# Bounded gathers, a deferred combination and repacked operands in a hybrid retention, S5 and mixture-of-experts block

## The chip, the cores and the metric

The kernel runs on one core of a Trainium2 chip. The metric is the device time of one execution in microseconds (us). The engines are PE (matrix products), DVE (vector), ACT (scalar functions and scaled copies), POOL (GpSimd) and SP, which only issues transfers; 16 DMA engines move the data. Each engine and each queue works its own list of instructions in order and waits on the others through semaphores.

## The reference, cut to what matters

512 tokens of width 2048, float32 throughout. A mixer (retention beside an S5 state space model) adds to x; a mixture of 32 experts adds to x; a gated projection (PLE) adds to x; a norm ends it.

```python
# S5: states of 64 groups of 16 channels, 64 complex states each
y = real(einsum('gcp,bsgp->bsgc', c_mat, states))
# router: 4 groups and 32 experts, 36 logits per token
g_prob = softmax(ht @ w_rg + b_rg);  e_logits = ht @ w_re + b_re
...
top_logit, top_j = lax.top_k(e_sel, 2)          # two experts of the best group
e_w = softmax(top_logit) * g_w
# each of the 1024 assignments goes through its expert
a = silu(xb @ w_gate[e]) * (xb @ w_up[e])        # 2048 -> 512
y = a @ w_down[e]                                # 512 -> 2048
out = segment_sum(y * row_w, row_tok)
# PLE
x = x + sigmoid(h @ w_ple_gate) * (p @ w_ple)
```

## The kernel before

Up to about 1350 us the program runs the mixer: dense products in three passes of split operands (L103, L104, L105: high by high, high by low, low by high; L62 on ACT makes the high part, L63 on DVE the low one), with the small products of the S5 part between them. `add_cross` (L467) multiplies the states xst of eight blocks of groups with the weights wb; xst holds chunk, part and group in that order, so one product reads every 64th element of a row.

The output projection goes over four blocks cb of 512 columns. After each, x is transposed (pt, L744), copied to SBUF (xt, L746, by ACT and DVE in turn), and multiplied by the router's weights wr (pl, L748), in two halves of 64 columns by parity of the piece. Each product of two float32 operands is two records in the trace and one row in the order of instructions.

Then the routing: `dispatch_ids` (L855 to L862) multiplies one-hot matrices ohd by token numbers (pq), so that each of the 128 slots of a pair of experts (64 each) holds its token number plus one, or zero where the slot is empty. The gather (L862, POOL) brings one row of 2048 numbers of x from HBM to each partition of xo; an empty slot brings row 0. `dispatch_scales` (L871) gives the weights sw, `dispatch_part` (px, L885) transposes xo into xg. Between these, PE makes the 32 products pw of p with w_ple, which wait for evacuation by ACT and a store to pw_d (L993 to L997).

The experts run in 16 pairs. Per expert, `load_expert` loads eight tiles of 1 MB for gate and up (L703) and four for down (L712) through SP's queue into 13 buffers mw and mwx, which are used in turn. `expert` makes pg (L1010; 64 slots by 512 columns, eight records per tile, in two halves of the array), sg on ACT and DVE (L1013 to L1015), pt and aT (L1018, L1020), py (L1026) and from it ysh on ACT and ysl on DVE (L1033, L1034), in split form. `combine` multiplies both by one-hot matrices (pc, L1049; 32 products for a pair), and DVE adds each result to x (L1050). The 16 px for the next pair stand in the first expert of a pair. The order on PE follows from a scheduler that knows the written order and the readiness of operands.

At the end `gate_w` (L1060 to L1068) loads and splits the first weights of the PLE gate: wh on ACT (L1066), wl on DVE (L1067), twelve times 128x512 each for the three tiles that are made early. A loop for experts with more than 64 tokens (L1105) follows, which begins with a branch on every engine, and then the PLE products (L1167 on).

## Time and profile before

| | us |
|---|---|
| median of 3 runs | 2581.95 (2581.84 to 2582.83) |
| profiled execution | 2583.66 |
| its span | 2581.9 |
| PE busy in the span | 2454.1 (95%) |
| DVE busy | 1128.8 (44%) |
| ACT busy | 570.2 (22%) |
| POOL busy | 133.6 (5%) |
| data moved | 626.41 MB, mean 243 GB/s |

The page's shares are means over stretches of different kinds; the table of stages among the rows below separates them. Ends of products are modelled, so the pace of PE is best read from the starts of neighbouring records.

### The profile page before, as it was taken

The page shows a single profiled execution, that of the slowest core. Times are in us where ns is not written, and L with a number is a line of the kernel's source. Part 1 is how long each engine was busy: PE and PEld are TensorE (multiplying, and loading weights), DVE is VectorE, ACT ScalarE, POOL GpSimd, SP SyncE. Part 2 cuts the span into 40 slices and gives each one's busy share as a digit, 9 for nine tenths or more (in the row PEclk, how much of TensorE's full clock was granted, in tenths as well). Part 3 has the DMA queues.
Part 4 walks back from the last instruction along what each step waited for, and adds up shares of the span by engine and source line. Part 5 has one row for each costly group of instructions (what it writes and reads, how often), then busy time and mean ns, then how long its engine had stood idle before and what let it go on. Part 6 is the DMA issues. An engine that isn't in the chain of part 4 may idle for free. (4 is left out here: it accounts for less than half of the span.)

```text
span 2581.9 us, 27822 instructions
## 1 busy us (share of the span) xinstructions
PE 2454.1 (95%) x11178; PEld 1595.3 (62%) x11178; DVE 1128.8 (44%) x2204; ACT 570.2 (22%) x722; POOL 133.6 (5%) x166
## 2 busy tenths in 40 slices
PE   8999999999999999999998999999999999997998
PEld 7888788888888888887763333333333333333886
DVE  6647966333443343542223344343333333334435
ACT  4242222231221232222221110000000000012534
POOL 1010000001101100000001000000000000000101
PEclk9999999999999999999999999999999999998999
DMA  8332333443323334653348999999999999995334
GB/s 300 110 99 90 120 117 103 152 161 104 106 90 98 104 124 148 224 218 114 116 172 344 421 420 421 420 420 421 420 421 421 420 420 421 421 420 231 104 118 147
DMA packets 168228, 626.41 MB, mean 243 GB/s; under 512 B 16402, under 2 KB 25106, under 8 KB 115490
## 3 DMA queue, kind: packets, MB, share of 16 engines
q1 hardware_dynamic: 160112, 597.22, 60.4%
q0 software_dynamic: 3376, 19.01, 1.8%
q10 hardware_dynamic: 4610, 8.39, 0.9%
q8 instruction: 89, 1.46, 0.2%
q14 instruction: 41, 0.34, 0.0%
HBM read 595.21 MB, written 29.43 MB: 242 GB/s over the span
## 5 line engine op out<-in xcount | busy, mean ns | idle before, releaser
L63 DVE TENSOR_TENSOR wl<-wst,wh 128x2048 fp32r<-128x2048 f32 (+1 forms) x111 | 251.6, 2267 | 410.7 <-ACT wh L62 410.5
L62 ACT ACTIVATE wh<-wst 128x2048 fp32r<-128x2048 f32 (+1 forms) x111 | 207.4, 1869 | 603.8 <-PE acc L104 359.1
L103 PE MATMUL acc<-hTh,wh 128*128 128x512 f32 x832 | 327.9, 394 | 11.2 <-ACT wh L62 6.8
L104 PE MATMUL acc<-hTl,wh 128*128 128x512 f32 x832 | 328.5, 395 | 0.0
L105 PE MATMUL acc<-hTh,wl 128*128 128x512 f32 x832 | 326.0, 393 | 0.3 <-DVE wl L63 0.2
L1010 PE MATMUL pg<-mw,xg 128*64 128x512 f32 x1040 | 259.6, 596 | 0.0
L1010 PE MATMUL pg<-mwx,xg 128*64 128x512 f32 x1008 | 250.6, 597 | 0.2 <-issue 0.2
L103 PEld LDWEIGHTS acc<-hTh,wh 128*128 128x128 f32 x832 | 157.1, 189 | 46.1 <-ACT wh L62 7.8
L1050 DVE TENSOR_TENSOR x<-pc,x 128x512 f32<-128x512 f32 x256 | 162.0, 685 | 41.0 <-PE pc L1049 40.7
L105 PEld LDWEIGHTS acc<-hTh,wl 128*128 128x128 f32 x832 | 157.3, 189 | 33.7 <-DVE wl L63 1.8
L104 PEld LDWEIGHTS acc<-hTl,wh 128*128 128x128 f32 x832 | 157.2, 189 | 32.9 <-issue 0.8
L1034 DVE SCALAR_TENSOR_TENSOR ysl<-py,sw,ysh 64x512 fp32r<-64x512 f32 x128 | 94.7, 749 | 175.5 <-ACT ysh L1033 170.8
L1010 PEld LDWEIGHTS pg<-mw,xg 128*64 128x64 f32 x1040 | 76.9, 137 | 139.9 <-issue 139.6
L1014 DVE SCALAR_TENSOR_TENSOR sg<-pg,sw,sg 128x256 f32<-128x256 f32 x32 | 15.5, 483 | 324.7 <-ACT sg L1013 324.7
L1010 PEld LDWEIGHTS pg<-mwx,xg 128*64 128x64 f32 x1008 | 73.7, 137 | 135.3 <-issue 135.1
L1033 ACT ACTIVATE ysh<-py,sw 64x512 fp32r<-64x512 f32 x128 | 87.3, 682 | 312.9 <-PE py L1026 298.4
L1026 PE MATMUL py<-mw,aT 128*64 128x512 f32 x616 | 147.3, 622 | 5.7 <-DVE aT L1020 5.7
L1013 ACT ACTIVATE sg<-pg,sw 128x256 f32<-128x256 f32 x32 | 15.1, 473 | 570.0 <-PE pg L1010 570.0
L1049 PE MATMUL pc<-ysh,oht 128*128 128x512 f32 x256 | 108.4, 433 | 29.1 <-ACT ysh L1033 22.3
L1049 PEld LDWEIGHTS pc<-ysh,oht 128*128 128x128 f32 x256 | 49.0, 192 | 100.6 <-DVE x L1050 54.5
L1049 PE MATMUL pc<-ysl,oht 128*128 128x512 f32 x256 | 101.7, 407 | 0.4 <-DVE ysl L1034 0.4
L103 PE MATMUL accp<-wh,h3h 128*128 128x512 f32 x256 | 101.6, 397 | 0.0
(354 smaller groups left out, 3618.9 us busy)
## 6 DMA issues: line engine op xcount, KB each, us to landing
mw<-in_w_exp_gu_dram SPq DMA_DIRECT2D x130, 1024.0 KB, 19.8
mwx<-in_w_exp_gu_dram SPq DMA_DIRECT2D x126, 1024.0 KB, 19.7
mw<-in_w_exp_down_dram SPq DMA_DIRECT2D x77, 1024.0 KB, 19.8
mwx<-in_w_exp_down_dram SPq DMA_DIRECT2D x51, 1024.0 KB, 19.8
wst<-in_w_in_dram SPq DMA_DIRECT2D x39, 1024.0 KB, 5.1
wst<-in_w_merge_dram SPq DMA_DIRECT2D x32, 1024.0 KB, 5.7
wst<-in_w_out_dram SPq DMA_DIRECT2D x16, 1024.0 KB, 5.3
wst<-in_w_ple_gate_dram SPq DMA_DIRECT2D x16, 1024.0 KB, 5.2
```

What stands on the lines that cost most here:

```text
L62: S.activation(hi, src, AF.Copy)
L63: V.tensor_sub(lo, src, hi.bitcast(FT))
L103: PE.matmul(acc, s0, m0, start=first, stop=False)
L104: PE.matmul(acc, s0, m1, start=False, stop=False)
L105: PE.matmul(acc, s1, m0, start=False, stop=last)
L1010: PE.matmul(pg[hf * 64:(hf + 1) * 64, :], xk, gu[kt // 2][:, kt % 2, :, hf * 256:(hf + 1) * 256], start=kt == 0, stop=kt == 15)
L1014: V.scalar_tensor_tensor(sg, pg[:, 0:256], rcol, sg, op0=OP.mult, op1=OP.mult)
L1026: PE.matmul(pys[c2][ch * 64:(ch + 1) * 64, :], aT[:, kc % 2, (kc // 2) * 64:(kc // 2 + 1) * 64], dn[kc][:, c0:c0 + 512], start=kc == 0, st ...
L1033: S.activation(yh[q, c0:c0 + 512], pys[c2][q], AF.Copy, scale=wcol[q])
L1034: V.scalar_tensor_tensor(yl[q, c0:c0 + 512], pys[c2][q], wcol[q], yh[q, c0:c0 + 512].bitcast(FT), op0=OP.mult, op1=OP.subtract)
L1049: PE.matmul(pc, oh[cb // 2][:, i * 128:(i + 1) * 128], ys[n][:, sl], start=n == 0, stop=n == 1)
L1050: V.tensor_tensor(x2[i][:, sl], pc, x2[i][:, sl], op=OP.add)
```

## The change

- `add_cross`: ACT copies the states of a block into contiguous xc, which the products then read.
- Router: wr is split into a high and a low part, side by side in 72 columns; x transposed is split too (ACT and DVE); eight products per block of 512 columns take the place of four of float32. The square for the norm is written over its input in PSUM.
- Gather: xo is one buffer, cleared once on POOL; an empty slot's index lies beyond a bound given to the gather, which is to leave out such rows.
- Experts: the combination of a pair is called in the middle of the next pair's first expert, the transposes of the next pair's rows in the middle of the second expert, and the scheduler places both among the other products.
- PLE: for the three early tiles ACT also scales the weights in place and POOL makes the difference; the last combination is written after them.
- The clearing of the routing table moves from the start to a later place on POOL.

```diff
+        xc = [t2k([128, BP, NCH], f"xc{i}") for i in range(2)]
+        for i in range(2):
+            S.activation(xc[i].rearrange("p j n -> p n j"), xst[:, 0:NCH, i, js], AF.Copy)
         py = ps("py")
         pyv = py.rearrange("p (j x) -> p j x", x=128)
         for jj in range(BP):
             for i in range(2):
-                PE.matmul(pyv[:, jj, :], wf[i][:, jj, :], xst[:, 0:NCH, i, j0 + jj], start=i == 0, stop=i == 1)
+                PE.matmul(pyv[:, jj, :], wf[i][:, jj, :], xc[i][:, jj, :], start=i == 0, stop=i == 1)
...
+    tini = glu.tile([128, (E * CAP + 2 * T) // 128, 4], FT, name="tini", bufs=1)
+    GP.memset(tini, 0.0)
+    GP.memset(tini[:, :, 0], -1.0)
+    GP.dma_start(tbl_d.rearrange("(p n) f -> p n f", p=128), tini)
...
-    wr = x1pool.tile([128, 16, 64], FT, name="wr", bufs=1)
-    GP.memset(wr[:, :, 36:], 0.0)
-    nc.sync.dma_start(wr[:, :, :36], A["w_router"])
-    GP.tensor_tensor(wr[:, :, :36], wr[:, :, :36], nffn[:, :, None].to_broadcast([128, 16, 36]), op=OP.mult)
+
+    wr = x1pool.tile([128, 16, 72], FR, name="wr", bufs=1)
+    wrf = wpool.tile([128, 4, 512], FT, name="wrf", tag="wst").rearrange("p k c -> p (k c)")[:, :576] \
+        .rearrange("p (d e) -> p d e", e=36)
+    nc.sync.dma_start(wrf, A["w_router"])
+    GP.tensor_tensor(wrf, wrf, nffn[:, :, None].to_broadcast([128, 16, 36]), op=OP.mult)
+    S.activation(wr[:, :, 0:36], wrf, AF.Copy)
+    V.tensor_tensor(wr[:, :, 36:72], wrf, wr[:, :, 0:36].bitcast(FT), op=OP.subtract)
...
-            jk = opool.tile([128, 512], FT, name="jk", tag="xt")
-            S.activation(jk, xn, AF.Square, accum_out=ss2[:, i, cb:cb + 1])
+            S.activation(p, xn, AF.Square, accum_out=ss2[:, i, cb:cb + 1])
...
-            xt = opool.tile([128, 512], FT, name="xt", tag="xt")
-            (S.activation(xt, pt, AF.Copy) if d % 2 else V.tensor_copy(xt, pt))
-            o = (d % 2) * 64
-            PE.matmul(pl[o:o + 64, :], wr[:, cb * 4 + d, :], xt, start=d < 2, stop=d >= 2)
+            xt = [opool.tile([128, 512], FR, name="x" + n, tag="x" + n) for n in "hl"]
+            split(pt, *xt)
+            for n in range(2):
+                PE.matmul(pl[:72], wr[:, cb * 4 + d, :], xt[n], start=d == n == 0, stop=d == 3 and n == 1)
...
+    xo = xtile([128, D], "xo", "xo")
+    GP.memset(xo, 0.0)
...
-        tk1 = mo.tile([128, 2], FT, name="tk1")
+        tk1 = mo.tile([128, 2], FT, name="tk1", bufs=3)
         V.tensor_reduce(tk1, pq[:, 0:4].rearrange("p (v n) -> p v n", v=2), axis=mybir.AxisListType.X, op=OP.add)
         oi = mo.tile([128, 1], I32, name="oi")
-        V.tensor_scalar(oi, tk1[:, 0:1], -1.0, 0.0, op0=OP.add, op1=OP.max)
-        xo = xtile([128, D], "xo", "xo")
+        none = mo.tile([128, 1], FT, name="none")
+        V.tensor_scalar(none, tk1[:, 0:1], 0.0, 2.0 * T, op0=OP.is_equal, op1=OP.mult)
+        V.scalar_tensor_tensor(oi, tk1[:, 0:1], -1.0, none, op0=OP.add, op1=OP.add)
         GP.indirect_dma_start(out=xo, out_offset=None, in_=x1_d,
-                              in_offset=bass.IndirectOffsetOnAxis(ap=oi[:, 0:1], axis=0))
+                              in_offset=bass.IndirectOffsetOnAxis(ap=oi[:, 0:1], axis=0),
+                              bounds_check=T - 1, oob_is_err=False)
...
+        if mid:
+            mid()
...
-        yh, yl = ys
+        yh, yl = ys()
...
+                if early:
+                    S.activation(st[:, k, :], st[:, k, :], AF.Copy, scale=sc)
+                    GP.tensor_tensor(wl[:, k, :], st[:, k, :], wh[:, k, :].bitcast(FT), op=OP.subtract)
+                    continue
...
     sw = sw0
+    last = None
     for pr in range(E // 2):
         _, xo, xg, tk1, _ = disp
         nxt, sw_n = disp, sw
-        ys = ytiles()
+        ys = []
+
+        def get_ys():
+            if not ys:
+                ys.extend(ytiles())
+            return ys
         for e in range(2):
             ee = pr * 2 + e
             wts = load_expert(wgu_a[ee], wd_a[ee]) if ee else first
+            for d4 in range(0 if ee else 4):
+                dispatch_part(xo, xg, d4)
             if e == 0 and pr + 1 < E // 2:
                 nxt = dispatch_ids(pr + 1)
                 sw_n = dispatch_scales(nxt[0], pr + 1)
 
             def xcol(kt):
-                if ee == 0 and kt % 4 == 0:
-                    dispatch_part(xo, xg, kt // 4)
                 return xg[:, kt, e * CAP:(e + 1) * CAP]
-            expert(wts, xcol, sw[:, e, 1:2], sw[:, e, 0:1], ys, e)
-            if e == 0 and pr + 1 < E // 2:
-                for d4 in range(4):
-                    dispatch_part(nxt[1], nxt[2], d4)
+
+            def mid():
+                if e == 0 and last:
+                    combine(*last)
+                if e == 1 and pr + 1 < E // 2:
+                    for d4 in range(4):
+                        dispatch_part(nxt[1], nxt[2], d4)
+            expert(wts, xcol, sw[:, e, 1:2], sw[:, e, 0:1], get_ys, e, mid)
         disp = nxt
         sw = sw_n
-        if pr == E // 2 - 1:
-            right = False
-            mwx.release()
-            x1pool.release()
-            ple = tc.alloc_tile_pool(name="ple", bufs=1, side="right", reuse_waits="tile")
-            pre = [gate_w(q, 0, q, mtile().rearrange("p (k c) -> p k c", k=4)) for q in range(3)]
-        combine(ys, [tk1[:, v:v + 1] for v in range(2)])
-
+        last = ys, [tk1[:, v:v + 1] for v in range(2)]
+    right = False
+    mwx.release()
+    x1pool.release()
+    ple = tc.alloc_tile_pool(name="ple", bufs=1, side="right", reuse_waits="tile")
+    pre = [gate_w(q, 0, q, mtile().rearrange("p (k c) -> p k c", k=4)) for q in range(3)]
+    combine(*last)
```

Line numbers move by the change: L1010 becomes L1022, L1018 L1032, L1026 L1040, L1034 L1048, L1049 L1063, L1050 L1064, L855 L864, L862 L872, L871 L882, L1066 L1081, L1067 L1084 (POOL).

On PE, in the experts, from the end of a pair's py, the order before was this (pc: combination of the pair that ends, pg: first expert of the next):

```order
L1049 MATMUL pc<-ysh,oht 128x512
L1010 MATMUL pg<-mwx,xg 64x512
L1049 MATMUL pc<-ysl,oht 128x512
L1049 MATMUL pc<-ysh,oht 128x512 x2
L1049 MATMUL pc<-ysl,oht 128x512 x2
L1049 MATMUL pc<-ysh,oht 128x512
L1049 MATMUL pc<-ysl,oht 128x512
L1049 MATMUL pc<-ysh,oht 128x512
L1049 MATMUL pc<-ysl,oht 128x512
L1049 MATMUL pc<-ysh,oht 128x512
L1049 MATMUL pc<-ysl,oht 128x512
L1010 MATMUL pg<-mwx,xg 64x512 x2
```

It is now this, with pq for the next gather ahead of py instead of among pg:

```order
L1040 MATMUL py<-mw,aT 64x512 x16
L1063 MATMUL pc<-ysh,oht 128x512
L1022 MATMUL pg<-mw,xg 64x512 x4
L1063 MATMUL pc<-ysl,oht 128x512
L1063 MATMUL pc<-ysh,oht 128x512
L1063 MATMUL pc<-ysl,oht 128x512
L1063 MATMUL pc<-ysh,oht 128x512
L1063 MATMUL pc<-ysl,oht 128x512
L1063 MATMUL pc<-ysh,oht 128x512
L1022 MATMUL pg<-mw,xg 64x512 x4
L1063 MATMUL pc<-ysl,oht 128x512
L1063 MATMUL pc<-ysh,oht 128x512
```

Single halves of a pg tile and runs of up to eleven pc have become whole tiles (four rows, eight records) with six pc between them.

On DVE, after the last expert, the order before was:

```order
L1034 SCALAR_TENSOR_TENSOR ysl<-py,sw,ysh 64x512 x3
L1067 SCALAR_TENSOR_TENSOR wl_14121<-mw,nple,wh_14120 128x512
L1034 SCALAR_TENSOR_TENSOR ysl<-py,sw,ysh 64x512
L1050 TENSOR_TENSOR x_7833<-pc,x_7833 128x512
L1067 SCALAR_TENSOR_TENSOR wl_14121<-mw,nple,wh_14120 128x512 x2
L1067 SCALAR_TENSOR_TENSOR wl_14133<-mw,nple,wh_14132 128x512 x3
L1050 TENSOR_TENSOR x_7833<-pc,x_7833 128x512
L1067 SCALAR_TENSOR_TENSOR wl_14133<-mw,nple,wh_14132 128x512
L1067 SCALAR_TENSOR_TENSOR wl_14145<-mw,nple,wh_14144 128x512 x3
L1067 SCALAR_TENSOR_TENSOR wl_14121<-mw,nple,wh_14120 128x512
```

On DVE it is now:

```order
L1048 SCALAR_TENSOR_TENSOR ysl<-py,sw,ysh 64x512 x3
L1064 TENSOR_TENSOR x_7865<-pc,x_7865 128x512
L1048 SCALAR_TENSOR_TENSOR ysl<-py,sw,ysh 64x512
L1064 TENSOR_TENSOR x_7865<-pc,x_7865 128x512 x3
L1064 TENSOR_TENSOR x_7866<-pc,x_7866 128x512 x4
L1064 TENSOR_TENSOR x_7867<-pc,x_7867 128x512 x4
L1064 TENSOR_TENSOR x_7868<-pc,x_7868 128x512 x4
L1131 TENSOR_LOAD ctl
```

And POOL, which had nothing there, has after its gathers:

```order
L872 DMA xo<-x_d,oi 128x2048 x15
L1084 TENSOR_TENSOR wl_14237<-mw,wh_14236 128x512 x2
L1084 TENSOR_TENSOR wl_14253<-mw,wh_14252 128x512 x2
L1084 TENSOR_TENSOR wl_14269<-mw,wh_14268 128x512 x2
L1084 TENSOR_TENSOR wl_14253<-mw,wh_14252 128x512
L1084 TENSOR_TENSOR wl_14237<-mw,wh_14236 128x512
L1084 TENSOR_TENSOR wl_14269<-mw,wh_14268 128x512
L1084 TENSOR_TENSOR wl_14253<-mw,wh_14252 128x512
L1084 TENSOR_TENSOR wl_14269<-mw,wh_14268 128x512
L1084 TENSOR_TENSOR wl_14237<-mw,wh_14236 128x512
```

The twelve subtractions wl have moved from between DVE's adds to POOL.

## Rows read from the trace of the kernel before

**Rows 1.** Stages: length, busy PE, PEld, DVE, ACT, POOL, clock, DMA share, GB/s

```profile
360.00:456.00 96.00, 96.00 (x424) 81.15 (x423) 58.39 (x98) 24.73 (x28) 0.00 (x0) 1.00 0.38 117
1450.00:2300.00 850.00, 777.22 (x3527) 294.07 (x3527) 317.37 (x557) 89.19 (x139) 15.24 (x13) 0.99 1.01 421
2358.00:2385.00 27.00, 13.69 (x41) 9.40 (x42) 20.95 (x34) 10.78 (x18) 0.00 (x0) 0.78 0.14 50
```

**Rows 2.** DMA, 1450 to 2300: total; software queue (packets, MB); gathers (issue to landing)

```profile
DMA packets 49053, 357.48 MB, mean 421 GB/s; under 512 B 5446, under 2 KB 5446, under 8 KB 5446
...
q0 software_dynamic: 1872, 13.63, 3.9%
...
xo<-x_d,oi POOLq DMA_INDIRECT x13, 10.4
```

**Rows 3.** Waits of SP's queue, 1450 to 2300: us, times, longest

```profile
SPq L703 <- PE pg L1010: 125.9, 96, 3.4
SPq L712 <- DMA mw<-in_w_exp_gu_dram: 98.9, 55, 3.1
```

**Rows 4.** POOL timeline, first and last gather of the stretch: start, length

```profile
1438.90 1.18 POOL L862 DMA_INDIRECT xo<-x_d,oi  x1 [63.46 <-PE pg L1010]
...
2252.36 1.17 POOL L862 DMA_INDIRECT xo<-x_d,oi  x1 [62.55 <-DVE oi L860]
```

**Rows 5.** PE timeline through one pair: start, length, work, count, idle before

```profile
1547.20 0.51 PE L1049 MATMUL pc<-ysh,oht 128*128 128x512 f32 x1 [1.49 <-ACT ysh L1033]
...
1551.35 1.08 PE L1010 MATMUL pg<-mw,xg 128*64 128x512 f32 x4
1552.36 0.50 PE L1049 MATMUL pc<-ysh,oht 128*128 128x512 f32 x1
...
1554.40 1.08 PE L1010 MATMUL pg<-mw,xg 128*64 128x512 f32 x4
...
1562.28 1.50 PE L1010 MATMUL pg<-mw,xg 128*64 128x512 f32 x5
...
1584.17 7.04 PE L1010 MATMUL pg<-mw,xg 128*64 128x512 f32 x32
1591.04 7.04 PE L1010 MATMUL pg<-mwx,xg 128*64 128x512 f32 x32
...
1600.70 3.65 PE L1026 MATMUL py<-mwx,aT 128*64 128x512 f32 x16 [0.52 <-DVE aT L1020]
...
1609.28 0.49 PE L1049 MATMUL pc<-ysh,oht 128*128 128x512 f32 x1 [1.49 <-ACT ysh L1033]
```

**Rows 6.** S5: PE timeline (strided L467, contiguous L421); line view of L422 (min/median/max ns)

```profile
365.01 3.65 PE L467 MATMUL py<-xst,wb 128*128 128x128 f32 x16
...
120.56 2.02 PE L421 MATMUL pS<-ut,m 128*128 128x128 f32 x16
...
L422 ACT ACTIVATE xst<-pS x16: 1047/1057/1160, 121.7 to 209.6; 128x512 f32<-128x512 f32 x16
```

**Rows 7.** Router: PE timeline around one run of L748

```profile
1187.62 1.43 PE L748 MATMUL pl<-xt,wr 128*64 128x512 f32 x4
1188.98 0.50 PE L104 MATMUL acc<-wl,m0h 128*128 128x512 f32 x1
```

**Rows 8.** Dispatch: PE timeline after the first routing weights

```profile
1361.67 10.32 PE L993 MATMUL pw<-mwx 128*128 128x512 f32 x18
```

**Rows 9.** After the experts: timelines of DVE, ACT, PE; POOL line L606

```profile
2366.21 4.06 DVE L1067 SCALAR_TENSOR_TENSOR wl<-mw,nple,wh 128x512 fp32r<-128x512 f32 x6
...
2376.44 3.17 DVE L1050 TENSOR_TENSOR x<-pc,x 128x512 f32<-128x512 f32 x5 [0.16 <-PE pc L1049]
...
2360.71 6.85 ACT L1066 ACTIVATE wh<-mw,nple 128x512 fp32r<-128x512 f32 x11
...
2383.35 3.51 PE L1167 MATMUL pt<-ident,x 128*128 128x128 f32 x16 [4.88 <-issue]
...
L606 POOL TENSOR_TENSOR yr<-yr,sg x8: 1273/1290/1297, 754.9 to 957.1; 128x512 f32<-128x512 f32 x8
```

More of the change, by code (lines that the diff above doesn't have):

```diff
@@ L55 @@
     tbl_d = dram.tile([(E + 2 * T // CAP) * CAP, 4], FT, name="tbl_d")
-    NT_ = (E * CAP + 2 * T) // 128
-    tini = const.tile([128, NT_, 4], FT, name="tini")
-    GP.memset(tini, 0.0)
-    GP.memset(tini[:, :, 0], -1.0)
-    GP.dma_start(tbl_d.rearrange("(p n) f -> p n f", p=128), tini)
     def split(src, hi, lo):
@@ L670 @@
     rs2 = const.tile([128, 4], FT, name="rs2")
-    opool = tc.alloc_tile_pool(name="opool", bufs=2, reuse_waits="tile")
+    opool = tc.alloc_tile_pool(name="opool", bufs=1, reuse_waits="tile")
     nffn = const.tile([128, 16], FT, name="nffn")
     nc.sync.dma_start(nffn, A["norm_ffn"])
-    wr = x1pool.tile([128, 16, 64], FT, name="wr", bufs=1)
-    GP.memset(wr[:, :, 36:], 0.0)
-    nc.sync.dma_start(wr[:, :, :36], A["w_router"])
-    GP.tensor_tensor(wr[:, :, :36], wr[:, :, :36], nffn[:, :, None].to_broadcast([128, 16, 36]), op=OP.mult)
+    wr = x1pool.tile([128, 16, 72], FR, name="wr", bufs=1)
[5 more added lines that the diff above has]
+    V.tensor_tensor(wr[:, :, 36:72], wrf, wr[:, :, 0:36].bitcast(FT), op=OP.subtract)
     br_ = x1pool.tile([128, 36], FT, name="br", bufs=1)
@@ L684 @@
     ss2 = x1pool.tile([128, 4, 4], FT, name="ss2", bufs=1)
-    lg = x1pool.tile([128, 512], FT, name="lg", bufs=1)
+    lg = x1pool.tile([128, 512], FT, name="lg", bufs=1)[:72]
     wgu_a, wd_a = A["w_exp_gu"], A["w_exp_down"]
@@ L744 @@
                 PE.transpose(pt[:, i * 128:(i + 1) * 128], x2[i][:, cb * 512 + d * 128:cb * 512 + (d + 1) * 128], ident)
-            xt = opool.tile([128, 512], FT, name="xt", tag="xt")
-            (S.activation(xt, pt, AF.Copy) if d % 2 else V.tensor_copy(xt, pt))
-            o = (d % 2) * 64
-            PE.matmul(pl[o:o + 64, :], wr[:, cb * 4 + d, :], xt, start=d < 2, stop=d >= 2)
+            xt = [opool.tile([128, 512], FR, name="x" + n, tag="x" + n) for n in "hl"]
+            split(pt, *xt)
+            for n in range(2):
+                PE.matmul(pl[:72], wr[:, cb * 4 + d, :], xt[n], start=d == n == 0, stop=d == 3 and n == 1)
         if cb == 0:
-            V.tensor_copy(lg, pl)
+            V.tensor_copy(lg, pl[:72])
         else:
-            V.tensor_tensor(lg, pl, lg, op=OP.add)
+            V.tensor_tensor(lg, pl[:72], lg, op=OP.add)
     V.tensor_reduce(rs2, ss2, axis=mybir.AxisListType.X, op=OP.add)
@@ L788 @@
     for i in range(4):
-        PE.transpose(plv[:, i, :], lg[:, i * 128:(i + 1) * 128], ident)
+        PE.transpose(plv[:, i, 0:72], lg[:, i * 128:(i + 1) * 128], ident[:72, :72])
     lt = rtile([128, 4, 36], "lt")
     lt2 = rtile([128, 4, 36], "lt2")
-    V.tensor_copy(lt2, plv[:, :, 64:100])
+    V.tensor_copy(lt2, plv[:, :, 36:72])
     V.tensor_tensor(lt, plv[:, :, 0:36], lt2, op=OP.add)
@@ L999, with expert @@
     mo2 = tc.alloc_tile_pool(name="mo2", bufs=1, reuse_waits="tile")
-    def expert(wts, xg, wcol, rcol, ys, swap):
+    def expert(wts, xg, wcol, rcol, ys, swap, mid=None):
         gu, dn = wts
@@ L1058, in gate_w @@
         with tc.high_priority(offset=4000 if st is None else 0):
-            if st is None:
+            early = st is not None
+            if not early:
                 st = wp2.tile([128, 4, 512], FT, name="wst", tag="wst")
@@ L1116 @@
             V.tensor_scalar(tko[g * 64:(g + 1) * 64, g:g + 1], tbo[g * 64:(g + 1) * 64, 0:1], 1.0, None, op0=OP.add)
-        xo = xtile([128, D], "xo", "xo")
+        xo = mtile()
         GP.indirect_dma_start(out=xo, out_offset=None, in_=x1_d,
@@ L1128 @@
             V.memset(y_.bitcast(FT), 0.0)
-        expert(wts, lambda kt: xgo[:, kt, 0:64], tbo[:, 1:2], tbo[:, 2:3], ys, 0)
+        expert(wts, lambda kt: xgo[:, kt, 0:64], tbo[:, 1:2], tbo[:, 2:3], lambda: ys, 0)
         combine(ys, [tko[:, v:v + 1] for v in range(2)])
```

## Prediction

> **What bounds the kernel now.** The table of stages comes first [rows 1]. The program has three kinds of stretch. Where dense products run, PE is full (96.00 of 96.00 us between 360 and 456) and the DMA engines are busy for a share of 0.38. In the expert stretch (1450 to 2300 and some 70 us on its two sides) the picture is another: DMA share 1.01, 421 GB/s, and PE at 777 of 850 us. After the last expert PE stands (13.69 of 27.00 us busy) while something else ends last.
>
> The expert stretch repeats a pair of experts 16 times. Its pace is read from POOL, which issues one gather per pair: 13 intervals between the first and the last gather shown make (2252.36 - 1438.90) / 13 = 62.57 us per pair [rows 4]. Two things come to nearly that length. **DMA**: 357.48 MB at a mean of 421 GB/s, over 850 / 62.57 = 13.58 pairs, is 26.3 MB, or 62.5 us, per pair; 13.63 MB of the total, 1.05 MB per gather, is the software queue, the gathers [rows 2]. **PE**: from the first pc of one pair to that of the next is 1609.28 - 1547.20 = 62.08 us [rows 5]. SP's queue, which issues the weight loads, waits in turn for buffers that PE frees and for landed transfers [rows 3]: neither leads by much. So a change of one of them alone gives little here, and this change touches both.
>
> **S5 cross term (add_cross).** PE reads xst with a stride of 256 bytes; 16 products take 3.65 us, while 16 of the same size from contiguous data (L421) take 2.02 [rows 6]. About 0.1 of the difference is the longer modelled end of the last one: 1.5 us for each of the 8 blocks, -12. PE has no gap in this stretch, so that counts in full. Added are 16 copies on ACT; the strided ACT instruction L422 takes 1.06 us, so 17 us on an engine that is busy 24.73 of 96 us there [rows 1, 6]. The copies stand in the queue in which ACT splits weights for the other products; if cover fails at two of the blocks for half a copy each, 1 us is lost. I take -11; the ends are -13 and, were a third of the copies exposed, -6.
>
> **Router.** A run of four records of L748 takes 1188.98 - 1187.62 = 1.36 us, 0.34 each [rows 7]; a block of 512 columns of x has eight, 2.7 us. The new form has eight products of 72 columns with the operand split in two. Their price isn't in the trace; a pg record, also 512 columns long, takes 6.87 / 32 = 0.215 [rows 5]: 1.7 us. Three of the four blocks stand in a full PE: 3 x 1.0 = -3. The split adds an ACT-DVE step ahead of each pair and the buffers are single; ends 0 and -5.
>
> **Dispatch, up to the first pg.** Two more of the 32 pw products run before the point where PE waits for routing weights, so 16 instead of 18 are left behind it, at 10.32 / 18 = 0.57 us [rows 8]: -1.1. The first gather brings half the rows; -0.4 for that. Against it, POOL now clears a 128x2048 buffer ahead of that gather. No such clearing is in the trace; the nearest POOL row is 1.29 us for 128x512 [rows 9], so at most 5. I take -1.5, ends -4 and +4.
>
> **Edits at nothing.** The clearing of the routing table moves to a later place on POOL, which is off the path and wholly idle in windows like that of 360 to 456 [rows 1]; the square jk written over its own input, the allocation of xo, three buffers for tk1 and the overflow loop's buffer (the loop runs zero times with this routing) change no wait that a row shows. 0.
>
> **Expert stretch, DMA side.** Routing the reference's own inputs gives 17 to 41 tokens per expert and 1024 tokens for 2048 slots, so half of each gather's rows are empty. If such rows move nothing, a pair has 0.52 MB less: 0.52 / 421 GB/s = 1.25 us, pace 61.3. Over 15 gathers that is -18.7.
>
> The DMA rate of that step is the row's 421 GB/s. The Trainium skill, DMA: Bandwidth & Descriptors, Specifications, puts the limit from HBM at about 358 GB/s per core and that of the fabric at 435; this case's rate is above the first, so the trace disagrees with it as a limit, and by 358 the same bytes would be worth 1.46 us per pair, 22 us in all.
>
> **Expert stretch, PE side.** Before, the 32 pc of the last pair lie in runs of up to eleven between single half tiles of pg. From the first pc to 1562.28, 15.08 us hold 32 pc, 18 records of pg and 16 small pq [rows 5]. One unit of eight pc and four pg takes 3.05 us (1551.35 to 1554.40); four such units and two pg at 0.215 would be 12.6, so 2.5 us go to lone rows and the pq. The new order (below the diff) makes six pc to one whole tile of eight pg. It has seven alternations where the units had four, each of at most 0.15 (four pg in 1.01 from 1551.35 to 1552.36, against 4 x 0.215) plus as much on the way back: +0.9. The 16 pq go behind pt of the second expert, where PE stood for 0.52 us until DVE had copied aT (the idle time at 1600.70); I let them stick out by 0.1. Sum -1.5, so 60.6. This pair was 0.5 shorter than the mean of 62.57; with the same 0.5 the mean becomes 61.1.
>
> DMA at 61.3 and PE at 61.1 are again close together, and of two streams that feed one another the slower sets the pace. I take 61.3: (62.57 - 61.3) x 16 pairs = **-20**. What the moves cost: the gather goes to POOL a whole expert earlier than it is used, the deferred combination holds its ys buffers until the next pair's first expert has its pg, and its adds on DVE run at 0.63 us (five in 3.17 [rows 9]), three per tile of six pc, or 1.9 us in some 3.2 of PE. So DVE keeps up. Ends: -26, if the reserve of landed weights is also used up at the end, and -4, below.
>
> **After the last expert.** DVE ran sixteen adds among twelve subtractions wl (six in 4.06, 0.68 us each) and ended last, 2376.44 + 3.17 = 2379.6; all engines meet at a branch and PE began at 2383.35 [rows 9]. Now DVE has only its adds, 16 x 0.63 = 10, and ends by about 2372. ACT has 24 copies instead of 12 at 0.62 (eleven in 6.85 from 2360.71), 15 us, ending near 2376. POOL has twelve subtractions at 1.29 (L606) [rows 9], from about 2361.3 to 2376.8; at 1.5 each it ends at 2379.3. POOL is thus the last, -2.8 or -0.3. I take -2.5, ends -7 (POOL not waited for) and +1.
>
> A rule of the Trainium skill speaks against this part: GPSIMD Engine Reference, Key points, says that for elementwise work DVE is about twice as fast as GpSimd. The rows agree (1.29 against 0.68), and by the rule alone twelve steps on POOL cost 7 us more than on DVE; it gains here only because DVE has the adds to do at the same time.
>
> **Sum.** -11 - 3 - 1.5 - 20 - 2.5 = -38. The profiled execution took 2583.66 us (span 2581.9), 1.7 over the median 2581.95. From the median: 2544.
>
> **Rivals.**
> 1. *Empty rows still cost their transfer*, the change not doing what it says: the descriptor is read, or written somewhere harmless. Then DMA stays at 62.5 per pair and PE's gain only eats into the weights' reserve, about 4 us: -22, so 2560. For it: no gather with a bound is in the trace. Against: an index beyond the bound has no row to read.
> 2. *PE's chain is not shorter.* The alternation six to one tile costs more per change than the rows show, or pc waits for DVE's adds at every tile. The stretch then stays at 62.5 and gives 0: -18, so 2564. For: each change between the two kinds costs, and there are more of them than in the units. Against: lone rows were the worst.
> 3. *Slower: the gather with a bound is slow software.* POOL handled a gather in 1.18 us and it landed 10.4 us after issue [rows 2, 4]. In the new order the pq that gives the index and the first px that uses it lie one py (1600.70 to 1609.28, 8.6 us) and one expert's pg with the 32 pc apart (2 x 6.87, and 12.2 - 16 x 0.215 = 8.8, [rows 5]), about 31 us. It decides when landing takes over 31 us; at 35 us each pair is 4 us longer than planned, 15 x 4 = 60, and 2544 + 60 = 2604. For: one index after the other may be compared in software. Against: that is three times the present time.
> 4. *POOL is too slow a place*: if it took 2 us per subtraction beside DVE's adds, it would end at 2385, +5 instead of -2.5: 2552. For: 1.29 is nearly twice DVE's 0.68. Against: L606 would have to become half as slow again. This is what the rule on GpSimd amounts to here.
>
> **How the numbers follow.** Forecast 0.55, first rival 0.15, second 0.13, third 0.06, fourth 0.05, others 0.06. The range takes in the first, second and fourth rival and, below, nearly all low ends together (-13 - 5 - 4 - 26 - 7 = -55, 2527): 2528 to 2565; the forecast's own is 2530 to 2556. About 0.2%, 5 us, is what a measurement of this kernel tells from no change. Slower by over 0.2%: 0.06; within 0.2%: 0.04; faster: 0.90.
>
> **What the profile of the changed kernel will show.** The 16 products of the S5 cross term in about 2.1 us. Software queue at half of 13.63 MB; a pace of gathers of 61.3 us with DMA still at 421 GB/s. No lone half tile of pg between pc, and waits of PE on weight landings that were not there before, since reserves shrink. After the last expert POOL as the last engine, 15 to 19 us after ACT's first copy of these weights. The forecast is wrong if gathers still move 1.05 MB, if DMA's rate falls below 421, or if pc rows wait for x on DVE.

## The result, and the profile after

The changed kernel takes 2540.93 us (median of 4 runs, 2535.57 to 2542.1) against 2582.39 for the kernel before (4 runs beside it): a ratio of 0.9835, 95% interval 0.9818 to 0.9852. The forecast was 2544 in 2528 to 2565. The profiled execution has a span of 2538.4 us, 43.5 less than before.

From the starts of the same products in the two traces:

| stretch, from start to start | before | after | change | forecast term |
|---|---|---|---|---|
| first product to first product on yTh (S5 within) | 517.9 | 507.6 | -10.3 | -11 |
| to first product on yh | 432.5 | 433.6 | +1.1 | 0 |
| to first product on m0h (branches) | 177.4 | 175.1 | -2.4 | 0 |
| to last product on m3h (three router blocks) | 191.1 | 186.2 | -5.0 | -3 |
| to first pg (dispatch) | 48.6 | 46.2 | -2.3 | -1.5 |
| to last py (experts) | 982.8 | 965.6 | -17.3 | -20 |
| to first product of PLE | 29.3 | 24.7 | -4.6 | -2.5 |
| to last product of PLE | 184.5 | 181.8 | -2.8 | 0 |

Before rounding the sum is -43.5, the whole of it: the two ends change by 0.3 each and cancel. The total lies 3 us below the forecast, but the terms miss by up to 3 us both ways, and two stretches that the forecast had put at 0, the branches and the PLE products, became shorter.

The DMA engines in the changed kernel, over 1450 to 2290 us (packets, MB; the software queue is the gathers):

```profile
DMA packets 49255, 352.34 MB, mean 419 GB/s; under 512 B 6276, under 2 KB 6276, under 8 KB 6276
...
q0 software_dynamic: 1872, 7.02, 2.1%
```

Beside [rows 2], 13.63 MB have become 7.02 with as many packets; the rate is 419 GB/s beside 421. POOL's timeline in the changed kernel (start, length, what, idle before), two of its gathers:

```profile
1577.53 0.99 POOL L872 DMA_INDIRECT xo<-x_d,oi  x1 [60.67 <-DVE oi L871]
...
2190.44 0.99 POOL L872 DMA_INDIRECT xo<-x_d,oi  x1 [59.62 <-DVE oi L871]
```

Ten intervals between these make 61.29 us on average, where [rows 4] gave 62.57. What SP's queue waited for in the changed kernel, 1450 to 2250 (us in total, times, longest):

```profile
SPq L718 <- DMA mw<-in_w_exp_gu_dram: 127.4, 56, 4.0
SPq L709 <- DMA mw<-in_w_exp_gu_dram: 117.4, 56, 2.1
SPq L709 <- DMA mw<-in_w_exp_down_dram: 116.0, 55, 2.5
...
SPq L709 <- PE pc L1063: 4.8, 16, 0.5
SPq L709 <- PE pg L1022: 3.0, 12, 0.4
```

In [rows 3] the largest wait was for PE's pg, 125.9 us; it is 3.0 now. Buffers are free before transfers have landed, so the DMA engines are full. That does not yet say that PE waits for them. PE's own waits for weights, 1450 to 2300:

```profile
PE pg L1022 <- DMA mw<-in_w_exp_gu_dram: 0.3, 1, 0.3
```

PE waited for a weight tile once, for 0.3 us. As far as the trace tells landings, the tiles came ahead of their first product by 7 us on average in pairs 2 to 4 and by 3 to 4 in pairs 10 to 14: DMA is a little the slower of the two, and PE lived on the reserve of landed tiles. One alternation on PE in the changed kernel:

```profile
1584.71 1.94 PE L1022 MATMUL pg<-mw,xg 128*64 128x512 f32 x8
1586.58 0.50 PE L1063 MATMUL pc<-ysl,oht 128*128 128x512 f32 x1
...
1588.17 1.94 PE L1022 MATMUL pg<-mw,xg 128*64 128x512 f32 x8
```

A tile of pg and six pc take 3.46 us (1584.71 to 1588.17), and no lone half is left, unlike in [rows 5].

### The profile page after: what moved, and what is told of

Read it like the earlier page. It is cut to its first block, busy times and chain, and to the rows that moved or that the text cites. A ratio compares the mean times of both kernels' runs of the same rounds, so it can differ in the third digit from the quotient of the medians.

```text
span 2538.4 us, 27924 instructions
## 1 busy us (share of the span) xinstructions
PE 2417.6 (95%) x11178; PEld 1576.3 (62%) x11178; DVE 1125.7 (44%) x2217; ACT 597.1 (24%) x759; POOL 147.9 (6%) x178
## 4 chain that ended last, share of the span: by engine, by line
PE 83%; DVE 6%; DMA 6%; ACT 3%; issue 1%; POOL 0%; SPq 0%; ACTq 0%; another core or an unknown queue 0%; POOLq 0%; DVEq 0%
PE pg L1022 16%; PE acc L100 13%; PE acc L99 13%; PE acc L98 13%; PE py L1040 9%; PE pc L1063 5%; DMA mw<-in_w_exp_gu_dram 2%; PE accp L98 2%; PE accp L100 2%; PE accp L99 2%; DMA mwx<-in_w_exp_down_dram 2%; PE px L896 1%; DVE wl L58 1%; DVE xst L437 1%; ACT ysh L1047 1%
## 5 line engine op out<-in xcount | busy, mean ns | idle before, releaser
L1022 PE MATMUL pg<-mw,xg 128*64 128x512 f32 x1040 | 238.5, 597 | 0.3 <-DMA mw<-in_w_exp_gu_dram 0.3
L1022 PE MATMUL pg<-mwx,xg 128*64 128x512 f32 x1008 | 231.0, 597 | 0.0
L1064 DVE TENSOR_TENSOR x<-pc,x 128x512 f32<-128x512 f32 x256 | 161.7, 684 | 129.7 <-PE pc L1063 129.6
L98 PEld LDWEIGHTS acc<-hTh,wh 128*128 128x128 f32 x832 | 156.8, 188 | 46.1 <-ACT wh L57 6.5
L1048 DVE SCALAR_TENSOR_TENSOR ysl<-py,sw,ysh 64x512 fp32r<-64x512 f32 x128 | 94.8, 750 | 170.9 <-ACT ysh L1047 166.1
L1040 PE MATMUL py<-mw,aT 128*64 128x512 f32 x616 | 153.0, 641 | 2.6 <-DVE aT L1034 1.5
L1022 PEld LDWEIGHTS pg<-mw,xg 128*64 128x64 f32 x1040 | 70.3, 136 | 136.0 <-issue 132.3
L1022 PEld LDWEIGHTS pg<-mwx,xg 128*64 128x64 f32 x1008 | 68.0, 136 | 131.8 <-issue 128.2
L1063 PE MATMUL pc<-ysh,oht 128*128 128x512 f32 x256 | 104.4, 408 | 22.5 <-ACT ysh L1047 22.4
L1026 DVE SCALAR_TENSOR_TENSOR sg<-pg,sw,sg 128x256 f32<-128x256 f32 x32 | 15.4, 483 | 223.7 <-ACT sg L1025 223.7
L1063 PE MATMUL pc<-ysl,oht 128*128 128x512 f32 x256 | 110.1, 431 | 0.4 <-DVE ysl L1048 0.4
L1040 PE MATMUL py<-mwx,aT 128*64 128x512 f32 x408 | 101.5, 639 | 0.8
```

What stands on the lines that cost most here:

```text
L98: PE.matmul(acc, s0, m0, start=first, stop=False)
L1022: PE.matmul(pg[hf * 64:(hf + 1) * 64, :], xk, gu[kt // 2][:, kt % 2, :, hf * 256:(hf + 1) * 256], start=kt == 0, stop=kt == 15)
L1040: PE.matmul(pys[c2][ch * 64:(ch + 1) * 64, :], aT[:, kc % 2, (kc // 2) * 64:(kc // 2 + 1) * 64], dn[kc][:, c0:c0 + 512], start=kc == 0, st ...
L1048: V.scalar_tensor_tensor(yl[q, c0:c0 + 512], pys[c2][q], wcol[q], yh[q, c0:c0 + 512].bitcast(FT), op0=OP.mult, op1=OP.subtract)
L1063: PE.matmul(pc, oh[cb // 2][:, i * 128:(i + 1) * 128], ys[n][:, sl], start=n == 0, stop=n == 1)
L1064: V.tensor_tensor(x2[i][:, sl], pc, x2[i][:, sl], op=OP.add)
```

## Experiments

The total of a single kernel scatters by some 5 us between runs here. Verdicts below therefore rest on ratios to the kernel before, run beside each kernel, and on stretches of the profiled executions where one stage is asked for. The stretch from first pg to last py scatters too: it takes 963.0 to 968.2 us in the eight runs with both halves of its change.

### The bytes and the order, each alone

One kernel keeps the new order and reads row 0 for every empty slot:

```diff
-        V.tensor_scalar(none, tk1[:, 0:1], 0.0, 2.0 * T, op0=OP.is_equal, op1=OP.mult)
-        V.scalar_tensor_tensor(oi, tk1[:, 0:1], -1.0, none, op0=OP.add, op1=OP.add)
+        V.tensor_scalar(oi, tk1[:, 0:1], -1.0, 0.0, op0=OP.add, op1=OP.max)
...
-                              bounds_check=T - 1, oob_is_err=False)
```

> The changed kernel, but empty slots point at row 0 again and the gather has no bound; the order on PE is that of the changed kernel row for row. Theory (the expert stretch is bound by the bytes that the DMA engines move): the software queue moves 1.05 MB per gather again, the pace of gathers returns from 61.3 to about 62.5 us, and the total is 15 x 1.25 = 18 us over the changed kernel, about 2559. Rival (the new order on PE made the gain, the bytes were hidden): pace 61.3 and total within 3 us of 2541.

The other is the kernel before with the bounded gather and its cleared buffer, and nothing else:

```diff
+    xo = xtile([128, D], "xo", "xo")
+    GP.memset(xo, 0.0)
...
-        V.tensor_scalar(oi, tk1[:, 0:1], -1.0, 0.0, op0=OP.add, op1=OP.max)
-        xo = xtile([128, D], "xo", "xo")
+        V.scalar_tensor_tensor(oi, tk1[:, 0:1], -1.0, none, op0=OP.add, op1=OP.add)
...
+                              bounds_check=T - 1, oob_is_err=False)
```

> The kernel before with only the bounded gather (one cleared buffer xo, empty slots beyond the bound); the order of the products stays that of before. Theory (PE's chain of 62.1 us, with its falls of the clock 62.6, sets the pace as soon as DMA's 61.3 is below it): pace of gathers 62.4 to 62.6, total within 4 us of the kernel before, 2578 to 2583. Rival (DMA alone was the bound): pace 61.3, total 18 us lower, 2564.

> The kernel before with only the bounded gather, and the first pair's px placed ahead of the second gather, which the first form of this edit had left behind it (there px waited 10.73 us for that gather). The order of the products of all later pairs stays that of before. Theory (PE's chain sets the pace once DMA is relieved): first pg to last py 983 us as before, pace 62.6 to 62.8, DMA below 420 GB/s, total within 4 us of the kernel before. Rival (the first form's 986 us came from its first pair, and the bytes are worth something alone): first pg to last py 970 or less.

In the first form of the second kernel the one buffer xo was filled by the second gather ahead of the first pair's px, so that the first pair worked on the second's rows; px waited 10.73 us and the ratio was 1.0046 (1.0029 to 1.0063). From first pg to last py it took 986.4 us. That wait is part of its total, hence the second form with px moved:

```diff
+            for d4 in range(0 if ee else 4):
+                dispatch_part(xo, xg, d4)
             if e == 0 and pr + 1 < E // 2:
...
-                if ee == 0 and kt % 4 == 0:
-                    dispatch_part(xo, xg, kt // 4)
```

| order of pc and px | empty rows | ratio to before (95%) | first pg to last py | software queue |
|---|---|---|---|---|
| before | read | 1 | 982.8 | 13.63 MB |
| before | left out | 0.9981 (0.9971 to 0.9990) | 983.2 | 7.02 MB |
| new | read | 0.9879 (0.9862 to 0.9895) | 982.5 | 13.63 MB |
| new | left out | 0.9835 (0.9818 to 0.9852) | 965.6 | 7.02 MB |

Neither half is worth anything in this stretch alone, within its scatter; together they bring 17 us (15 to 20 over the runs with both). That the kernel with the new order and all rows is faster in total comes from the other parts of the change, which it has too. What binds is seen in the two halves' own rows. The new order with all rows read, DMA and SP's queue, 1450 to 2250:

```profile
DMA packets 46065, 335.72 MB, mean 420 GB/s; under 512 B 5113, under 2 KB 5113, under 8 KB 5113
...
q0 software_dynamic: 1872, 13.63, 4.1%
```
```profile
SPq L718 <- DMA mw<-in_w_exp_gu_dram: 135.7, 56, 4.0
...
SPq L709 <- PE pg L1019: 5.8, 23, 0.4
```

And PE's waits for weights in that kernel, 1450 to 2300:

```profile
PE pg L1019 <- DMA mwx<-in_w_exp_gu_dram: 8.2, 15, 1.1
PE pg L1019 <- DMA mw<-in_w_exp_gu_dram: 7.2, 16, 0.6
```

The old order with empty rows left out (second form), DMA over 1450 to 2300, SP's queue over 1450 to 2250:

```profile
DMA packets 49333, 352.87 MB, mean 415 GB/s; under 512 B 6289, under 2 KB 6289, under 8 KB 6289
```
```profile
SPq L703 <- PE pg L1015: 283.8, 151, 9.4
...
SPq L712 <- DMA mw<-in_w_exp_gu_dram: 22.9, 12, 2.1
```

With the old order the queue waits for PE's buffers and the rate falls below 420: PE's chain sets the pace. PE has no wait for weights there, nor has it one in the kernel before. With the new order and all rows the queue waits for landings and PE waits 15.4 us for weights, nearly the whole 17: DMA sets the pace. Both rivals fall: in the new order the bytes were not hidden, and in the old order DMA was not the bound.

### The next bound

The changed kernel without the gathers of pairs 1 to 15:

```diff
-        GP.indirect_dma_start(out=xo, out_offset=None, in_=x1_d,
+        if pr == 0:
+            GP.indirect_dma_start(out=xo, out_offset=None, in_=x1_d,
```

> The changed kernel without the gathers of pairs 1 to 15: these pairs work on the rows of the first, everything else is done. This shows the next bound. Weights alone are 25.17 MB per pair, 59.9 us at 420 GB/s. Theory (DMA is the only bound of the changed kernel, and PE's chain, read from its first pairs, is shorter than 60): pace 59.9, so the total falls by 15 x 1.3 = 20 us to 2521. Rival (PE at 60.6 plus falls of the clock, 61.1, stands right behind): the total falls by 3 to 6 us only, 2535 to 2538.

First pg to last py is 961.5 us, only 4 less, and the ratio 0.9817 (0.9801 to 0.9834), which can't be told from the changed kernel's. The rival holds. SP's queue, 1450 to 2250:

```profile
SPq L709 <- PE pg L1023: 306.8, 156, 3.5
...
SPq L718 <- DMA mw<-in_w_exp_gu_dram: 32.8, 20, 2.1
```

PE leads again as soon as 0.52 MB per pair are gone. From the second pt of one pair to that of the next its undisturbed pairs take 60.1 us and its others 61.8, with a mean of 60.9; the forecast had put PE at 61.1. So DMA at 61.3 needs some 0.4 us a pair more than PE.

The mix is not as I had thought. Before, 62.0 was the undisturbed pair and one in three took 63.7. The new order saves 1.9 on an undisturbed pair, more than the 1.5 of the forecast, but most pairs are now disturbed by a fall of PE's clock. The changed kernel has the same two lengths, 60.1 and mostly 61.6 to 61.8, besides two pairs of 62.0. One of the disturbed pairs in the changed kernel, in steps of 2 us (length, busy PE, PEld, DVE, ACT, POOL, granted clock, DMA share, GB/s):

```profile
1818.00:1820.00 2.00, 0.57 (x4) 0.00 (x0) 0.84 (x2) 0.47 (x1) 0.00 (x0) 1.00 1.05 434
1820.00:1822.00 2.00, 1.59 (x20) 1.01 (x22) 1.41 (x6) 0.00 (x0) 0.00 (x0) 0.74 0.98 410
1822.00:1824.00 2.00, 2.00 (x8) 0.66 (x6) 0.28 (x2) 0.00 (x0) 0.98 (x1) 0.50 1.01 422
1824.00:1826.00 2.00, 2.00 (x12) 0.61 (x10) 0.00 (x0) 0.00 (x0) 0.01 (x1) 0.90 1.02 422
```

PE stands for 1.4 of two us while sg is made, and then the clock is at the lower of its two levels (0.50 of full, 1.2 GHz) for some 3.4 us. Read in such steps of 2 us, this happened at six places between 1450 and 2330 before and at twelve between 1500 and 2320 after. PE stands like this in every expert, and the clock fell after some of these stands only; why more often now was not tried.

This decides how the 4 us are read. PE's instructions are the same, one by one, in the changed kernel and in the one without gathers; from first pg to last py their clock falls 12 and 10 times. Two falls at 1.7 us (61.8 less 60.1) are 3.4 of the 4.1 us, which leaves 0.7 for the gathers. So in this execution PE's chain with its falls, and not DMA, held the stretch. Another run with the same order and the same bytes (the version with the shared differences and the moved buffer, at the end of this section) has only 7 falls, and PE waits for weights ten times, 4.8 us in all: its stretch is 965.7. The two bounds lie so close that the number of falls decides which of them is felt.

### S5 operand

```diff
-        xc = [t2k([128, BP, NCH], f"xc{i}") for i in range(2)]
-        for i in range(2):
-            S.activation(xc[i].rearrange("p j n -> p n j"), xst[:, 0:NCH, i, js], AF.Copy)
...
-                PE.matmul(pyv[:, jj, :], wf[i][:, jj, :], xc[i][:, jj, :], start=i == 0, stop=i == 1)
+                PE.matmul(pyv[:, jj, :], wf[i][:, jj, :], xst[:, 0:NCH, i, j0 + jj], start=i == 0, stop=i == 1)
```

> The changed kernel with the S5 cross term as before: PE reads the strided states, no copies on ACT. Theory (a strided operand slows these 128 records): 3.65 us per 16 again and the total 9 to 12 us higher, 2550 to 2553. Rival (the copies' waits take the gain back): within 4 us of 2541.

The ratio goes back to 0.9855 (0.9838 to 0.9871), 2550.69 us; its interval still meets that of the changed kernel, so the stretch decides. From the first to the last of these 128 records it is 88.3 us, as before; in the changed kernel 78.4. Sixteen records of the changed kernel, and what its line waited for (us, times):

```profile
364.44 1.95 PE L465 MATMUL py<-xc,wb 128*128 128x128 f32 x16
366.14 0.48 PE L98 MATMUL acc<-hTh,wh 128*128 128x512 f32 x1
```
```profile
  ACT xc L460: 5.9, 10
  issue: 1.0, 2
  DVE wb L346: 0.9, 2
```

1.70 us from start to start, where the strided form needed 3.3, the 3.65 of [rows 6] less its modelled end. 8 x 1.6 would be 12.8, and 9.9 came. The waits show where most of the rest went. The 5.9 us count the same wait on the weight loads and on the products; the products alone stood 2.1 us, ahead of six of the eight blocks, 1.2 of it for the copies.

### Router

```diff
-            xt = [opool.tile([128, 512], FR, name="x" + n, tag="x" + n) for n in "hl"]
-            split(pt, *xt)
-            for n in range(2):
-                PE.matmul(pl[:72], wr[:, cb * 4 + d, :], xt[n], start=d == n == 0, stop=d == 3 and n == 1)
+            xt = opool.tile([128, 512], FT, name="xt", tag="xt")
+            (S.activation(xt, pt, AF.Copy) if d % 2 else V.tensor_copy(xt, pt))
+            o = (d % 2) * 64
+            PE.matmul(pl[o:o + 64, :], wr[:, cb * 4 + d, :], xt, start=d < 2, stop=d >= 2)
```

> The changed kernel with the router's products in float32 as before. Between the first products of two output blocks each router block cost 1.67 us less in the changed kernel. Theory (the float32 records of half width cost that): three blocks 5 us longer, total 2545 to 2547. Rival (the gain there came from the square written in place or from the pace of neighbours): within 1.5 us of 2541.

The stretch over three blocks takes 190.2 us instead of 186.2 (total 2545.29). Of the 5.0 us gained, 4.0 come back with this edit; the square in place stays changed here, and may hold the other 1.0, which was not tried apart. The whole (0.9838, 0.9822 to 0.9854) can't be told from the changed kernel. Two of the new products in the changed kernel, beside [rows 7]:

```profile
1173.04 0.40 PE L753 MATMUL pl<-xl,wr 128*72 128x512 f32 x1
1173.27 0.39 PE L100 MATMUL acc<-wh,m0l 128*128 128x512 f32 x1
...
1173.73 0.39 PE L753 MATMUL pl<-xh,wr 128*72 128x512 f32 x1
```

They stand singly between dense products, 0.23 us from start to start (1173.04 to 1173.27), without the long slot that a pair of float32 records had to itself (0.98 to 1.00 us from the first of two to the next other product, in the float32 form).

### After the last expert

```diff
-                if early:
-                    S.activation(st[:, k, :], st[:, k, :], AF.Copy, scale=sc)
-                    GP.tensor_tensor(wl[:, k, :], st[:, k, :], wh[:, k, :].bitcast(FT), op=OP.subtract)
-                    continue
```

> The changed kernel with the early PLE splits as before: ACT makes wh only, and DVE makes the twelve differences among its adds. Theory (all engines meet at the branch, and DVE with adds and differences ends last): from the last py to the first pt of PLE 26 us instead of 21.3, total 4 to 5 us over the changed kernel, 2545. Rival (the gain there came from elsewhere, such as the clock): within 1.5 us of 2541.

The stretch takes 29.5 us again instead of 24.7; the total, 2543.88 (0.9842, 0.9826 to 0.9859), can't be told from the changed kernel. A shared form leaves nine differences on POOL and puts three behind DVE's adds:

```diff
+                if early and k == 3:
+                    late.append((wl[:, k, :], st[:, k, :], sc, wh[:, k, :].bitcast(FT)))
+                    continue
...
     combine(*last)
+    for o_, a_, sc_, b_ in late:
+        V.scalar_tensor_tensor(o_, a_, sc_, b_, op0=OP.mult, op1=OP.subtract)
```

> The changed kernel, but of the twelve early differences nine stay on POOL and the last of each tile goes to DVE behind its adds, without ACT's scaled copy. Theory (POOL ends last there, at 1.3 to 1.4 us each, 6.9 us after DVE's last add): POOL ends 4 us earlier and so does the branch; total 3 to 4 us under the changed kernel, 2537. Rival (ACT's queue or the clock decides): within 1.5 us of 2541.

It takes 22.6 us, 2.1 less than the changed kernel and short of the 4 expected; the total is 2535.48 (0.9809, 0.9793 to 0.9826). The ends in the three, first the changed kernel's POOL, DVE, ACT and PE:

```profile
2331.89 9.86 POOL L1084 TENSOR_TENSOR wl<-mw,wh 128x512 fp32r<-128x512 f32 x8 [0.58 <-POOL wl L1084]
...
2325.75 9.19 DVE L1064 TENSOR_TENSOR x<-pc,x 128x512 f32<-128x512 f32 x15
...
2342.02 0.63 ACT L1204 ACTIVATE jk<-x 128x512 f32<-128x512 f32 x1 [3.53 <-POOL wl L1084]
...
2342.14 3.67 PE L1195 MATMUL pt<-ident,x 128*128 128x128 f32 x16 [8.80 <-POOL wl L1084]
```

Then the form with all differences on DVE:

```profile
2341.78 0.63 ACT L1200 ACTIVATE jk<-x 128x512 f32<-128x512 f32 x1 [12.34 <-DVEq L1129]
...
2345.41 3.41 PE L1191 MATMUL pt<-ident,x 128*128 128x128 f32 x16 [5.24 <-issue]
```

And the shared form:

```profile
2331.63 4.63 POOL L1088 TENSOR_TENSOR wl<-mw,wh 128x512 fp32r<-128x512 f32 x3
2331.98 1.94 ACT L1082 ACTIVATE wh<-mw,nple 128x512 fp32r<-128x512 f32 x3
2332.72 4.09 DVE L1134 SCALAR_TENSOR_TENSOR wl<-mw,nple,wh 128x512 fp32r<-128x512 f32 x3 [0.53 <-ACT wh L1082]
...
2337.40 3.47 PE L1200 MATMUL pt<-ident,x 128*128 128x128 f32 x16 [6.80 <-DVEq L1138]
```

POOL is the last in the changed kernel (2341.75), as forecast, and 12 of its steps fit into 16.7 us; in the shared form DVE ends last at 2336.8, half a microsecond after POOL. Part of what was missing there shows in its rows: DVE's three differences took 4.09 us, where six took 4.06 before [rows 9], and POOL's three beside them 4.63. The two slowed each other: two of DVE's three steps last 1.75 us instead of 0.75, and the two of POOL's that overlap them 1.70 to 1.74 instead of 1.27. DVE's adds, which read pc from PSUM, keep their 0.68 beside POOL. The larger part of the gain of the changed kernel is another: in the changed and the shared form PE starts as ACT does, 0.1 to 0.2 us apart, in the kernel before and in the form with all differences on DVE it starts 3.4 to 3.6 us after ACT. This is taken up below.

### The clearing of the table, and where operands lie

```diff
+    NT_ = (E * CAP + 2 * T) // 128
+    tini = const.tile([128, NT_, 4], FT, name="tini")
+    GP.memset(tini, 0.0)
...
-    tini = glu.tile([128, (E * CAP + 2 * T) // 128, 4], FT, name="tini", bufs=1)
```

> The changed kernel with the clearing of the routing table back at the start, in a buffer that stays for the whole program; no other instruction changes, but buffers allocated later lie at other addresses. The branch products (L98 to L100 on yh) took 177.4 us of start-to-start before and 175.0 after, and the PLE products 187.2 and 184.7, with the same records at the same granted clock, some of them at 0.238 us instead of 0.227. Theory (the place of the operands in memory sets that pace): these stretches go back towards 177.4 and 187.2, total 2 to 5 us over the changed kernel, 2543 to 2546. Rival (it varies from run to run, or the S5 copies did it): both stretches as after, total within 1.5 us of 2541.

> The changed kernel with three of the twelve early differences on DVE behind its adds, as in the run before that did so, and with the buffer for the cleared table allocated behind the yT buffers instead of ahead of them, which moves yT by 384 bytes per partition. Theory (the relative place of the operands sets the pace of these products): the 192 records on yTh go from 0.2333 back to 0.2267, 1.2 us, and with the 2.1 us of the shared differences the total is 3 us under the changed kernel. Rival (only the weights' place counts): yTh stays at 0.2333, 2 us under.

```diff
-    tini = glu.tile([128, (E * CAP + 2 * T) // 128, 4], FT, name="tini", bufs=1)
...
         yTs.append((hi, lo))
+    tini = glu.tile([128, (E * CAP + 2 * T) // 128, 4], FT, name="tini", bufs=1)
```

> The changed kernel itself, on the same chip and in the same hours as the next one. Its total should be 0.983 to 0.985 of the kernel before; last py to first accp of PLE 24.7 us, yTh products 0.233 us apart.

Start of the first and of the last of these products, line view, in the changed kernel:

```profile
L98 PE MATMUL acc<-yh,wh x256: 388/389/476, 947.8 to 1122.1; 128*128 128x512 f32 x128
...
L98 PE MATMUL acc<-yTh,wh x64: 392/394/398, 514.1 to 558.2; 128*128 128x512 f32 x64
```

With the clearing back at the start:

```profile
L103 PE MATMUL acc<-yh,wh x256: 389/390/477, 946.4 to 1123.2; 128*128 128x512 f32 x128
...
L103 PE MATMUL acc<-yTh,wh x64: 389/389/389, 514.3 to 557.2; 128*128 128x512 f32 x64
```

And with the buffer behind yT, and the shared differences:

```profile
L98 PE MATMUL acc<-yh,wh x256: 389/389/475, 947.8 to 1122.5; 128*128 128x512 f32 x128
...
L98 PE MATMUL acc<-yTh,wh x64: 389/389/389, 515.7 to 558.5; 128*128 128x512 f32 x64
```

The products on yh take 174.3, 176.8 and 174.7 us, those on yTh 44.1, 42.9 and 42.8; before it was 176.7 and 42.9. No instruction on PE differs among these three but for the addresses of its buffers. The products on yh lose their gain when the clearing goes back, the products on yTh lose their penalty when only that small buffer moves. Both answers repeat: the changed kernel run again gives 174.7 and 44.1, and so do, within 0.3 us, the six other runs that leave this buffer where the change has it. With the clearing at the start the total is 2542.71 (0.9831, 0.9814 to 0.9848), which can't be told from the changed kernel.

The PLE products do not fit. They took 184.5 us before, 181.8 after and 185.0 with the clearing at the start, but 184.3 in the changed kernel run again, with the same addresses. That -2.8 is no effect that I can hold on to; it varies between executions.

The version with both, 2535.13 us (2534.96 to 2538.65), stands at 0.9804 (0.9791 to 0.9818) beside the changed kernel's 2541.68 (2537.46 to 2542.89) and 0.9819 (0.9806 to 0.9832) on the same chip. The medians differ by 6.5 us; the intervals overlap. The yTh products give 1.2 and the branch 2.1 of it by the traces. Its dispatch stretch was 43.3 us against 46.1; in the runs with the new order this stretch takes 43.2 to 46.2.

## Why the prediction was right or wrong

**S5, -11: right.** 9.9 between the first and the last of these records. The gain per block was as read (1.6), and the waits lost 2.9 us where I had allowed 1.

**Router, -3: mis-sized, -5.0.** I priced runs of four and left out that a lone pair of float32 records takes 1.0 us, 0.49 each, not 0.34. The difference for one block is 1.7, not 1.0; the run in the float32 form shows 1.3 of it.

**Dispatch, -1.5: right in size (-2.3), not shown in cause.** This stretch differs by up to 3 us between runs that have the same work there, and it is 2.5 us shorter with the bounded gather alone as well, 3.6 with the new order and all rows; so the term can't be told from that. The clearing of xo on POOL, for which I had only a bound of 5 us, took 1.81 and stood 36 us ahead of the first gather, while POOL was idle:

```profile
1299.00 1.81 POOL L850 MEMSET xo<- 128x2048 f32 x1 [200.20 <-PE acc L100]
...
1335.16 1.10 POOL L872 DMA_INDIRECT xo<-x_d,oi  x1 [0.46 <-DVE sl L812]
```

**Edits at nothing: wrong.** The step said that moving the table's clearing changes no wait. It changes no wait, but it moves buffers: -2.4 on the stretch of the branches and +1.2 on yTh.

**Experts, -20: the pair of edits right, the size -17.3, the bound in part luck.** That a change of one side alone gives little was the forecast's strongest statement, and the two halves bear it out: 0 each, 17 together. But the step that lets DMA set the new pace fits this execution only by its number. The pace of 61.29 meets the forecast's 61.3, yet it is made mostly of pairs near 60.1 and 61.7, with two of 62.0. The first two lengths are PE's own, without and with a fall of the clock, as the kernel without gathers has them. PE's gain was mis-sized, 1.9 on an undisturbed pair and not 1.5, and twice as many falls took much of it back; its mean of 60.9 lands beside the forecast's 61.1. The term also took 16 pairs, where there are 15 gathers to save, 18.7 us by the DMA side; the runs with both halves gave 15 to 20. Rivals 1 and 2 fall (7.02 MB; 60.1 us in an undisturbed pair). So do rival 3 (the gather's busy time on POOL stayed near 1 us, it landed after 9.3 us in the median, and no px waited) and rival 4 (a difference on POOL took 1.23 us, not 2).

**The signs.** Halved gathers, 61.3 us, no lone half tile and POOL as last engine after the experts came, the last 18.9 us after ACT's first copy, and the 16 products of the S5 term in 1.95 us. The waits of PE on landings did not: 0.3 us in all. And the sign that was to speak against the forecast, a rate below 421 GB/s, came by its letter with 419; it says little, since the rate is then the bytes of a pair over a pace to which PE's chain comes as near as DMA.

**The rate and the rule on HBM.** Where DMA is full, 419 to 421 GB/s were moved, before and after. The Trainium skill (DMA: Bandwidth & Descriptors, Specifications) gives about 358 GB/s as the limit from HBM per core; the trace disagrees with it as a limit here.

**After the last expert, -2.5: right sign, -4.6.** POOL ends 1.4 us earlier than DVE had ended, relative to the last py; I had 2.8. The other 3.2 us is PE's late start after the branch, which I had taken as a constant (the 3.7 us between DVE's end and PE's start in [rows 9]). The shared form, which uses both engines, is the best of the three. The Trainium skill (GPSIMD Engine Reference, Key points) puts DVE at about twice GpSimd's speed for elementwise work; the trace agrees in the price per step, 0.68 us against 1.23, which did not decide the end here.

**The sum** came out within 3 us of the forecast because the router, PE's start after the branch and the moved buffers gave back what the experts and S5 fell short of, and because of 2.8 us of the PLE products that are no effect of the change as far as the runs show. That these cancel so well is luck.

## What to carry to other kernels

Where two resources have nearly the same pace, test each saving with the other undone: here two edits worth 0 were worth 17 us as a pair, and the run without gathers says that a next step would again need both. The queue of the transfers shows whether DMA is full: it then waits for landings, not for products. Whether that costs anything is read from PE's own waits for tiles, 15.4 us with all rows and 0.3 without the empty ones. A small buffer that moves can change the pace of dense products elsewhere by 3%, so an edit that issues nothing on an engine isn't an edit at nothing.
